# Operands of the second token half four steps sooner, early squares on ScalarE, and half an operand set loaded behind the weights

## The chip, the core and the metric

The kernel runs on one core of a Trainium2 chip. The metric is the time of one execution on the device in microseconds (us); a kernel's time is the median of its runs. The profile is of one execution of its own.

## The reference

One layer of a decoder trunk in float32, 1024 tokens, width 1024. Four token mixers (convolution, latent attention, pooling, gated spatial mixing) and an output projection give the residual `h`; all of this lies ahead of the change. What the change touches is the dense part behind it:

```
f = jnp.square(jax.nn.relu(rms_norm(h, ffn_norm_g) @ w_ff1))    # 1024 x 4096
h = h + f @ w_ff2                                               # 4096 x 1024
return rms_norm(h, final_norm_g)
```

## The kernel before

**Products.** Both matrix products are done by a scheme with seven products of half-size blocks instead of eight. A pair is 2 x 128 of the 4096 features (16 pairs); the tokens are cut in two halves of 512. For each pair the products P1 to P7 take one weight operand (`a11`, `a12`, `a21`, `a22` or sums of them, made in place by `sum1` to `sum4`) and one token operand: B11 and B21 (first half of the tokens), T1, B22, T2, T3, T4 (these need the second half). Each float32 operand is split into a high and a low part: ScalarE copies the high one (rounded to the matmul's type), VectorE subtracts for the low one, and a product is three matmul passes, so a step on TensorE is 4 x 3 = 12 matmuls of 128x512.

**Steps.** `run` writes the order of all engines out by hand. In iteration k it emits, in this order: the weight loads of step k+8 (SyncE), what follows step k-1 (`post`), the operand splits of step k+4 (`prep`), the extra work hung on step k (`now`), the second half of what follows step k-1 (`split`), and the matmuls of step k. Each engine runs its part of that list strictly in order. What lies ahead of step 0 is ordered by a planner and interleaves with the first steps.

**Phase one, early products.** Steps 0 to 23 are P1 (`one[p]`, step 2p-1) and P2 (`two[p-1]`, step 2p) of pairs 0 to 11, which need only the first token half, while the second half is still being finished. After `one[p]` ScalarE copies the bank out (`m1`, L980) and GpSimd's queue stores it; `two[p]`, three steps later, accumulates onto the same bank and so waits for that copy. After `two[p]`, `f_relu` takes Relu on ScalarE (L949), the square on VectorE (L951), stores `fe` to `fr`, and `f_parts` splits it into `fst` (L130, L131) and stores that to `fs` (L958). The tile `fst` is one single buffer ("CS") for pairs 0 to 2 and one of the ten weight slots (`w`) for pairs 3 to 11.

**Second-half operands.** They are hung on steps as `now` work, for j = 0 to 3: `hn_T1` at 7 + 2j (8 transposes on TensorE, L793; one ScalarE and four VectorE operations, L810 to L815), `hn_T1_split` at 8 + 2j (L825, L827: two copies, two subtractions), `combine` at 15 + 2j (two VectorE operations, L832, L833) and `combine_split` at 16 + 2j (three copies, three subtractions; the last copy takes the buffer that the third operand's source gives up). `h_away` at step 5 stores `h[4..7]` to HBM on SyncE's queue.

**The rest of phase one.** Step 24 is P5 of pair 0, step 25 P6, step 26 P3; P3 accumulates onto P5's bank and waits for ScalarE's copy `s5` of it, whose buffer ("N") held the last `fe`. Then come the other products of pairs 0 to 11, and all seven of pairs 12 to 15. The last seven steps (`tail`: P1, P5, P6, P2, P7, P3, P4 of pair 15) and the seven before them (`tail2`) also issue the first loads of phase two.

**Phase two.** Four chunks of four pairs, each with seven products M1, M2, M4, M6, M5, M7, M3 of four steps. Left operands are the stored parts `fop` 0, 1, 3 (from `fs`; M1, M2 and M4) or splits of the stored `f1`, `f2` (from `fr`); right operands are the second weights `w1`, `w2`. A step of M1 takes all four operands of a set. After each step VectorE adds the bank to `h` (`add_h`, L1083). The first loads, in SyncE's order, are `fop` 1, the last `w1`, `fop` 0, `w2`, `f1`, `f2`, then, hung on M2, `fop` 3.

The functions that the diff touches:

Of the kernel before, what the change touches and what calls it, by code (L numbers as in the profile page):

```python
# [11 lines left out]
AF = mybir.ActivationFunctionType  # L12
# [51 lines left out]
def trunk_kernel(tc, a):  # L64
    nc = tc.nc
    act = nc.scalar
    dve = nc.vector
    pool = nc.gpsimd
    pe = nc.tensor
    with (  # L70
        tc.tile_pool(name="sb", bufs=1) as sb,
        tc.tile_pool(name="ps", bufs=1, space=bass.MemoryType.PSUM) as ps,
        tc.tile_pool(name="hbm", bufs=1, space=bass.MemoryType.DRAM) as hbm,
    ):
        _trunk(tc, nc, act, dve, pool, pe, sb, ps, hbm, a)


def _trunk(tc, nc, act, dve, pool, pe, sb, ps, hbm, a):
# [25 lines left out]
    def wslot(name):  # L104
        return sb.tile([P, 1024], F32R, tag="w", name=name, bufs=2 * NW)

    def M(name, shape):
        return sb.tile([P] + shape, F32, tag="M", name=name, bufs=NM)
# [7 lines left out]
    def X(name):  # L116
        return ps.tile([P, 1024], F32, tag="X", name=name, bufs=2)
# [144 lines left out]
    b = X("zc")  # L262
# [40 lines left out]
    for i, hf in ((1, 0), (0, 1), (1, 1)):  # L303
        if (i, hf) == (0, 1):
            ba, bg = K("zc"), O("zc")
        else:
            b = X("zc")
# [37 lines left out]
    for i in range(2):  # L345
        w = load_w(a["w_cm"][4 + i], 1024, "wp%d" % i)
        b = X("zp")
# [434 lines left out]
    def split_to(t, src):  # L782
        split(t[:, 0], t[:, 1], src)
        return t
# [56 lines left out]
    def mm_half(b, w, name, start):  # L841

        for j in range(KH):
            mm3(b, lambda x: w[:, x, j * P:(j + 1) * P], lambda y: hb[name, j][:, y, :],
                start and j == 0, j == KH - 1, not start)

    def slot(name):
        return wslot(name).rearrange("p (x c) -> p x c", x=2)
# [4 lines left out]
    def E(name):  # L853
        return sb.tile([P, 512], F32, tag="e", name=name, bufs=1)
# [84 lines left out]
    def f_store(p, q, f):  # L939
        pool.dma_start(fr[p][q // 2][:, (q % 2) * 512:(q % 2 + 1) * 512], f)  # L940

    def f_sum(p, q, b, s):

        dve.tensor_add(s, b, s)  # L944
        dve.scalar_tensor_tensor(s, s, 0.0, s, ALU.max, ALU.mult)
        f_store(p, q, s)

    def f_relu(p, q, b, f, mul):
        act.activation(f, b, AF.Relu)  # L949
        if mul:  # L950
            dve.tensor_mul(f, f, f)  # L951
        else:
            act.activation(f, f, AF.Square)
        f_store(p, q, f)

    def f_parts(p, q, f, t):
        split_to(t, f)
        pool.dma_start(fs[p][q], t.rearrange("p x c -> p (x c)").bitcast(F32))  # L958

    def set_bank(b):  # L960

        pe.matmul(b, hb["B11", 0][:, 0, 0:P], hb["B11", 0][:, 0, :], start=True, stop=True)

    class Pair:
# [18 lines left out]
        def early(self):  # L983
            p = self.p
            o1, o2 = self.op("a11"), self.op("a12")

            def one():
                self.bx = (W, K, W, O)[p % 4]("ffe")
                mm_half(self.bx, o1.t, "B11", True)

            def one_post():
                self.keep("m1", lambda n: M(n, [512]), self.bx)
                pool.dma_start(m1[p], self.m1)

            def two():
                mm_half(self.bx, o2.t, "B21", False)

            def two_post():
                self.f = (N if p % 2 else E if p < NEARLY - 4 else spare)("fe")
                f_relu(p, 0, self.bx, self.f, True)  # L1000

            def two_split():
                f_parts(p, 0, self.f, slot("fst") if p > 2 else
                        sb.tile([P, 2, 512], F32R, tag="CS", name="fst", bufs=1))

            return (Step(one, [o1, o2], loads=[lambda: self.load(0)], post=one_post),
                    Step(two, post=two_post, split=two_split))
# [24 lines left out]
        def steps(self):  # L1032
            p, whole = self.p, self.p >= NEARLY
            S = {}

            def product(name, wop, bank, tok, start, **kw):
                o = self.op(wop)
                S[name] = Step(lambda: mm_half(bank(), o.t, tok, start), [o], **kw)

            def y0():  # L1040
                self.by = (K, O)[p % 2]("ffy")
                return self.by

            def x():
                return self.bx

            def z_seed():
                self.bz = X("ffz")[:, 0:512]
                if p < NEARLY + 2:
                    set_bank(self.bz)  # L1050
                act.activation(self.bz, self.bx, AF.Copy)

            def two_post():
                self.f11 = E("f11")
                f_relu(p, 0, self.bz, self.f11, False)

            def four_post():
                self.f21 = M("f21", [512])
                f_relu(p, 1, self.bx, self.f21, False)

            load = [lambda: self.load(0, "H"), lambda: self.load(1)]
            if whole:
                product("P1", "a11", x, "B11", True, loads=load, pre=self.banks, post=z_seed, sums=[self.sum1])
                load = []
                product("P2", "a12", lambda: self.bz, "B21", False, sums=[self.sum4], post=two_post,
                        split=lambda: f_parts(p, 0, self.f11, slot("fst")))
            product("P5", "a21", y0, "T1", True, loads=load, sums=[self.sum2],
                    post=lambda: self.keep("s5", (N, spare)[p % 2], self.by))
            product("P6", "a11", x, "T2", False, sums=[] if whole else [self.sum4],
                    post=lambda: self.keep("s2", lambda n: M(n, [512]), self.bx))  # L1070
            product("P3", "a12", lambda: self.by, "B22", False, sums=[] if whole else [self.sum3],
                    post=lambda: f_sum(p, 2, self.by, self.s2))
            product("P7", "a21", x, "T3", False, post=lambda: f_sum(p, 3, self.bx, self.s5),
                    split=lambda: f_parts(p, 3, self.s5, slot("fst")))
            product("P4", "a22", x, "T4", False, post=four_post, split=lambda: f_parts(p, 1, self.f21, slot("fst")))
            if whole:
                S["P2"].sums.append(self.sum3)
            self.S = S
# [393 lines left out]
    steps = [one[0]]  # L1472
# [1 line left out]
        steps += [one[p], two[p - 1]]  # L1474
    steps.append(two[-1])
    for j in range(KH):
        for f, s in ((hn_T1, 7 + 2 * j), (hn_T1_split, 8 + 2 * j), (combine, 15 + 2 * j), (combine_split, 16 + 2 * j)):
            steps[s].now.append(lambda j=j, f=f: f(j))
    steps[5].now.append(h_away)
    for p in pairs:  # L1480
        p.steps()

# [3 lines left out]
    for p in range(NPAIR):  # L1486
        s, nx = pairs[p].S, pairs[p + 1].S if p + 1 < NPAIR else {}
# [13 lines left out]
        pairs[p - 1].S["P7"].now.append(pairs[p].seed)  # L1501
    tail, tail2 = steps[-7:], steps[-14:-7]
    c0 = chunks[0]
    for t, n, name, ii in ((tail2, 1, "w1", (0, 1)), (tail2, 5, "w1", (2,)), (tail, 1, 1, range(4)),
                           (tail, 2, "w1", (3,)), (tail, 2, 0, range(4)), (tail, 3, "w2", range(4)),
                           (tail, 5, "f1", range(4)), (tail, 6, "f2", range(4))):
        t[n].now += [c0.ld(name, i) for i in ii]
    for n in range(4):
# [119 lines left out]
```

## Time and profile before

| | |
|---|---|
| time, median of 3 runs | 1042.67 us (1041.95 to 1043.56) |
| the profiled execution's own time | 1039.44 us |
| its span, first to last instruction | 1037.70 us |
| granted TensorE clock, mean | 0.985 |
| TensorE busy | 992.7 us |
| VectorE busy | 846.3 us |
| ScalarE busy | 502.3 us |
| TensorE waits and slow steps, 391 to 475 us | 2 long waits (3.61 and 2.79 us), one step at half clock |
| TensorE waits, 711 to 727 us | 0.43 and 1.93 us |

The profiled execution lies 3.23 us under the median; sums are made against it and then moved to the median. PE is TensorE, DVE VectorE, ACT ScalarE, POOL GpSimd, SP SyncE. A matmul is listed with its whole latency (0.39 us), while the next starts 0.23 us later.

### The profile page before, as it was taken

What the parts mean: (1) busy time and instruction counts of PE and PEld (TensorE: products, weight loads), DVE (VectorE), ACT (ScalarE), POOL (GpSimd) and SP (SyncE); (2) the same over time, 40 slices, a digit from 0 to 9 for tenths busy, and PEclk for the clock granted to TensorE, in tenths of its full rate; (3) what the DMA queues carried; (4) which work ended last, traced back from release to release, by engine and by line L of the source; (5) the groups of instructions that cost most, each with busy time, mean ns of one, the idle gap of its engine ahead of it and who ended that gap; (6) DMA issues with size and microseconds to landing.
All of it is one profiled execution on the core that took longest, in us unless ns stands there. A gap on an engine that the chain in (4) does not pass through costs nothing.

```text
span 1037.7 us, 13384 instructions
## 1 busy us (share of the span) xinstructions
PE 992.7 (96%) x4674; PEld 817.8 (79%) x4674; DVE 846.3 (82%) x1276; ACT 502.3 (48%) x937; POOL 246.8 (24%) x333
## 2 busy tenths in 40 slices
PE   9994899999999999988999999999999999999996
PEld 7883689888888887867888887887888888888885
DVE  5999999998888765987677775656998988988997
ACT  7641147556657765754545444453341431431424
POOL 0459558423232312222121111211000000000005
PEclk9997899999999999999999999999999999999998
DMA  9411015210002006866666675559858258258004
GB/s 334 165 56 37 32 54 185 82 41 23 19 1 82 1 1 216 298 246 219 235 217 230 233 235 185 220 181 414 337 189 298 82 181 306 81 180 326 1 1 163
DMA packets 49492, 165.71 MB, mean 160 GB/s; under 512 B 6032, under 2 KB 7952, under 8 KB 49424
## 3 DMA queue, kind: packets, MB, share of 16 engines
q1 hardware_dynamic: 36288, 119.68, 33.1%
q0 software_dynamic: 12992, 45.10, 11.1%
q8 instruction: 37, 0.61, 0.2%
q14 instruction: 31, 0.25, 0.1%
q10 hardware_dynamic: 144, 0.07, 0.0%
HBM read 113.45 MB, written 51.38 MB: 159 GB/s over the span
## 4 chain that ended last, share of the span: by engine, by line
PE 65%; DVE 16%; issue 6%; DMA 5%; ACT 4%; POOL 3%; SPq 0%; POOLq 0%; DVEq 0%; ACTq 0%
PE ffb L160 16%; PE ffx L160 13%; PE ffa L160 12%; DVE acc L337 8%; PE ffy L160 8%; PE wo L160 4%; PE ob L160 2%; PE s L676 2%; PE zc L160 2%; DMA raw_b<-in_w_ff 2%; DMA fs<-fst 1%; PE ptb L719 1%; PE woa L160 1%; PE qb L160 1%; DVE h L475 1%
## 5 line engine op out<-in xcount | busy, mean ns | idle before, releaser
L160 PE MATMUL ffb<-wop,fop 128*128 128x512 f32 x756 | 178.3, 395 | 0.0
L160 PEld LDWEIGHTS ffb<-wop,fop 128*128 128x128 f32 x756 | 142.1, 188 | 34.2
L160 PE MATMUL ffx<-hnT,wop 128*128 128x512 f32 x624 | 149.4, 392 | 0.8 <-DVE s L944 0.8
L160 PE MATMUL ffa<-wop,fop 128*128 128x512 f32 x576 | 137.3, 397 | 2.4 <-DVE h L1083 1.9
L160 PEld LDWEIGHTS ffx<-hnT,wop 128*128 128x128 f32 x624 | 117.0, 188 | 27.2 <-DVE s L944 1.2
L884 DVE TENSOR_TENSOR wop<-w_raw,wop 128x512 fp32r<-128x512 f32 x112 | 76.1, 688 | 68.3 <-ACT wop L881 68.3
L160 PEld LDWEIGHTS ffa<-wop,fop 128*128 128x128 f32 x576 | 109.2, 190 | 28.6 <-DVE h L1083 2.4
L881 ACT ACTIVATE wop<-raw_b 128x512 fp32r<-128x512 f32 x96 | 59.6, 623 | 122.9 <-PE ffa L160 44.3
L337 DVE SCALAR_TENSOR_TENSOR acc<-ycv,cols,acc 128x512 f32<-128x512 f32 (+22 forms) x100 | 99.1, 1032 | 0.7 <-ACT acc L317 0.4
L881 ACT ACTIVATE wop<-w_raw 128x512 fp32r<-128x512 f32 x112 | 68.8, 626 | 43.8 <-DVE w_raw L1027 18.9
L881 ACT ACTIVATE fop<-raw_f 128x512 fp32r<-128x512 f32 x64 | 39.8, 623 | 74.7 <-DVE h_back L1083 27.6
L160 PE MATMUL ffe<-hnT,wop 128*128 128x512 f32 x288 | 70.5, 402 | 4.4 <-ACT m L980 4.4
L1243 POOL TENSOR_SCALAR mr_ms<-mssq,epsr 128x1 f32<-128x1 f32 x7 | 2.8, 401 | 296.9 <-ACT fjunk L1241 296.9
L884 DVE TENSOR_TENSOR wop<-raw_b,wop 128x512 fp32r<-128x512 f32 x96 | 65.6, 684 | 9.3 <-ACT wop L881 8.6
L160 PEld LDWEIGHTS ffe<-hnT,wop 128*128 128x128 f32 x288 | 54.4, 191 | 17.0 <-ACT m L980 5.2
L160 PE MATMUL ffy<-hnB,wop 128*128 128x512 f32 x192 | 46.9, 393 | 2.8 <-ACT s L980 2.8
L160 PE MATMUL ffy<-hnT,wop 128*128 128x512 f32 x192 | 46.6, 391 | 0.0
L958 POOL DMA_DIRECT2D fs<-fst x48 | 25.8, 538 | 87.1 <-DVE fst L131 83.7
L160 PEld LDWEIGHTS ffy<-hnB,wop 128*128 128x128 f32 x192 | 36.0, 188 | 11.3 <-ACT s L980 3.2
L884 DVE TENSOR_TENSOR fop<-raw_f,fop 128x512 fp32r<-128x512 f32 x64 | 43.9, 686 | 0.0
L160 PEld LDWEIGHTS ffy<-hnT,wop 128*128 128x128 f32 x192 | 36.2, 189 | 8.1
L329 POOL TENSOR_TENSOR acc<-acc,tap 128x512 f32<-128x512 f32 (+7 forms) x20 | 35.0, 1749 | 28.9 <-ACT tap L328 27.6
(453 smaller groups left out, 2157.2 us busy)
## 6 DMA issues: line engine op xcount, KB each, us to landing
fs<-fst POOLq DMA_DIRECT2D x48, 512.0 KB, 3.4
fop<-fs SPq DMA_DIRECT2D x48, 512.0 KB, 7.2
w_raw<-in_w_ff SPq DMA_DIRECT2D x44, 512.0 KB, 4.4
raw_b<-in_w_ff SPq DMA_DIRECT2D x32, 512.0 KB, 5.9
raw_f<-fr SPq DMA_DIRECT2D x32, 512.0 KB, 5.7
fr<-s POOLq DMA_DIRECT2D x32, 256.0 KB, 3.2
fr<-f POOLq DMA_DIRECT2D x20, 256.0 KB, 2.4
xin<-in_x SPq DMA_DIRECT2D x8, 512.0 KB, 8.7
```

The source lines that it names most:

```text
L160: pe.matmul(out, lhs(x), rhs(y), start=start and i == 0, stop=stop and i == 2, skip_group_check=more)
L329: pool.tensor_tensor(aa, aa, tap, ALU.add)
L337: dve.scalar_tensor_tensor(aa, ya, c, aa, ALU.mult, ALU.add)
L475: dve.scalar_tensor_tensor(h[t], b, rs, h[t], ALU.mult, ALU.add)
L676: pe.matmul(sb_[:, c0:c0 + w], q[:, x, qo:qo + P], kt[:, y, 0:w], start=i == 0, stop=i == 2 and not last)
L719: pe.transpose(b[:, place[j] + s * P:place[j] + (s + 1) * P], pts[s][:, (2 * kp + j) * P:(2 * kp + j + 1) * P], ident)
L881: act.activation(self.t[:, 0], self.src(), AF.Copy)
L884: dve.tensor_sub(self.t[:, 1], self.src(), high(self.t))
L958: pool.dma_start(fs[p][q], t.rearrange("p x c -> p (x c)").bitcast(F32))
L1243: pool.tensor_scalar(ms, ssq, epsr[:, t:t + 1], 1.0, ALU.add, ALU.mult)
```

## The change

1. `f_relu` squares on ScalarE always; VectorE's multiplication (early pairs) goes.
2. `hn_T1` and `hn_T1_split` hang on steps 3 + 2j and 4 + 2j, `combine` and `combine_split` on 12 + 2j and 13 + 2j; `h_away` on step 4.
3. `fst` takes a weight slot from pair 1 on; only pair 0 uses "CS".
4. Of the four `fop` 1 loads, two are issued where all four were (`tail` step 1), two behind the four `w2` loads (`tail` step 3).

```
-    def f_relu(p, q, b, f, mul):
+    def f_relu(p, q, b, f):
         act.activation(f, b, AF.Relu)
-        if mul:
-            dve.tensor_mul(f, f, f)
-        else:
-            act.activation(f, f, AF.Square)
+        act.activation(f, f, AF.Square)
         f_store(p, q, f)
...
-                f_parts(p, 0, self.f, slot("fst") if p > 2 else
+                f_parts(p, 0, self.f, slot("fst") if p else
                         sb.tile([P, 2, 512], F32R, tag="CS", name="fst", bufs=1))
...
-        for f, s in ((hn_T1, 7 + 2 * j), (hn_T1_split, 8 + 2 * j), (combine, 15 + 2 * j), (combine_split, 16 + 2 * j)):
+        for f, s in ((hn_T1, 3 + 2 * j), (hn_T1_split, 4 + 2 * j), (combine, 12 + 2 * j), (combine_split, 13 + 2 * j)):
             steps[s].now.append(lambda j=j, f=f: f(j))
-    steps[5].now.append(h_away)
+    steps[4].now.append(h_away)
...
-    for t, n, name, ii in ((tail2, 1, "w1", (0, 1)), (tail2, 5, "w1", (2,)), (tail, 1, 1, range(4)),
-                           (tail, 2, "w1", (3,)), (tail, 2, 0, range(4)), (tail, 3, "w2", range(4)),
+    for t, n, name, ii in ((tail2, 1, "w1", (0, 1)), (tail2, 5, "w1", (2,)), (tail, 1, 1, (0, 1)),
+                           (tail, 2, "w1", (3,)), (tail, 2, 0, range(4)), (tail, 3, "w2", range(4)), (tail, 3, 1, (2, 3)),
                            (tail, 5, "f1", range(4)), (tail, 6, "f2", range(4))):
```

The callers of `f_relu` drop the last argument.

## Rows read from the trace of the kernel before

**Rows 1.** The page's first part: busy time, share of the span and instructions of each engine.

```profile
PE 992.7 (96%) x4674; PEld 817.8 (79%) x4674; DVE 846.3 (82%) x1276; ACT 502.3 (48%) x937; POOL 246.8 (24%) x333
```

**Rows 2.** Busy time by stretch: the stretch, its length, then busy us (and instructions) of each engine, TensorE's granted clock as a share of 2.4 GHz, the share of time that the DMA engines are busy, and GB/s. The two stretches are phase one behind the early products.

```profile
475.00:691.00 216.00, 215.22 (x938) 175.64 (x937) 145.41 (x225) 108.11 (x186) 41.49 (x77) 1.00 0.62 217
691.00:711.80 20.80, 20.80 (x92) 17.02 (x91) 13.23 (x21) 9.69 (x17) 4.30 (x8) 1.00 0.88 336
```

**Rows 3.** TensorE's timeline in the early products and the first two steps behind them: start, us from the first start to the last end, line, operation, what it writes and reads, how many, and in brackets the idle time before it and what ended it.

```profile
394.96 14.10 PE L160 MATMUL ffe<-hnT,wop 128*128 128x512 f32 x60 [0.74 <-ACT m L980]
408.90 1.04 PE L793 MATMUL htb<-ident,h 128*128 128x128 f32 x8
...
415.30 1.03 PE L793 MATMUL htb<-ident,h 128*128 128x128 f32 x8
...
428.88 27.85 PE L160 MATMUL ffe<-hnT,wop 128*128 128x512 f32 x120
460.35 4.62 PE L160 MATMUL ffe<-hnT,wop 128*128 128x512 f32 x12 [3.61 <-ACT m L980]
464.80 2.92 PE L160 MATMUL ffy<-hnT,wop 128*128 128x512 f32 x12
...
473.27 2.99 PE L160 MATMUL ffy<-hnB,wop 128*128 128x512 f32 x12 [2.79 <-ACT s L980]
```

**Rows 4.** Busy time by stretch, one microsecond behind the wait at 460.35 (columns as in rows 2; the granted clock is the 0.50).

```profile
462.00:463.00 1.00, 1.00 (x4) 0.81 (x3) 1.00 (x3) 0.06 (x1) 0.43 (x1) 0.50 0.16 62
```

**Rows 5.** The waits of 385 to 480 us: who waited, for whom; us in total, times, the longest.

```profile
ACT hnT L825 <- DVE hnT L827: 8.5, 4, 2.7
...
ACT fst L130 <- DMA fs<-fst: 6.7, 2, 5.1
```

**Rows 6.** VectorE's timeline, 385 to 478 us: the same operations of two neighbouring pairs, the two weight splits in the `hn_T1` stretch (L884) and the early `f_relu` in the combine stretch (L951).

```profile
419.90 1.29 DVE L884 TENSOR_TENSOR wop<-w_raw,wop 128x512 fp32r<-128x512 f32 x2
...
426.16 1.29 DVE L884 TENSOR_TENSOR wop<-w_raw,wop 128x512 fp32r<-128x512 f32 x2
...
444.41 0.68 DVE L951 TENSOR_TENSOR fe<-fe 128x512 f32<-128x512 f32 x1
...
450.74 0.69 DVE L951 TENSOR_TENSOR fe<-fe 128x512 f32<-128x512 f32 x1
```

**Rows 7.** TensorE's timeline at the start of phase two: M1 (`ffa`), then M2 and M4 (`ffb`).

```profile
711.82 2.20 PE L160 MATMUL ffa<-wop,fop 128*128 128x512 f32 x9
714.45 3.67 PE L160 MATMUL ffa<-wop,fop 128*128 128x512 f32 x15 [0.43 <-DMA fop<-fs]
720.04 7.36 PE L160 MATMUL ffa<-wop,fop 128*128 128x512 f32 x24 [1.93 <-DVE h L1083]
727.24 22.56 PE L160 MATMUL ffb<-wop,fop 128*128 128x512 f32 x96
```

**Rows 8.** The chain of work that ended last, 690 to 780 us: start, us, what.

```profile
700.46 16.22 DMA raw_b<-in_w_ff
...
719.24 0.76 DVE h L1083
```

**Rows 9.** ScalarE's timeline, 711.9 to 713.4 us: Relu and Square of a pair outside the early products, which already run there.

```profile
712.01 0.60 ACT L949 ACTIVATE f<-ffx 128x512 f32<-128x512 f32 x1 [1.88 <-PE ffx L160]
712.65 0.63 ACT L953 ACTIVATE f<-f 128x512 f32<-128x512 f32 x1
```

**Rows 10.** ScalarE's timeline, 385 to 478 us: the last scaling of an `h` tile of the second half, and two independent weight copies one behind the other.

```profile
396.33 1.15 ACT L757 ACTIVATE h<-h,rs 128x1024 f32<-128x1024 f32 x1
...
444.15 1.14 ACT L881 ACTIVATE wop<-w_raw 128x512 fp32r<-128x512 f32 x2
```

**Rows 11.** The DMA issues of the whole span: what, queue, operation, how many, KB of each, median us from issue to landing.

```profile
hs<-h SPq DMA_DIRECT2D x4, 512.0 KB, 10.6
```

**Rows 12.** The tile `fs` from 401 to 419 us: the three stores of `fst` that are issued there (pairs 0 to 2).

```profile
DMA to landing us min/median/max: 5.0/5.2/7.9
```

**Rows 13.** The chain of work that ended last, 300 to 560 us: the store of the last early pair.

```profile
469.37 3.15 DMA fr<-fe
```

**Rows 14.** Busy time by stretch at the start of phase two (columns as in rows 2; the last two are the DMA engines' share and GB/s).

```profile
694.00:697.00 3.00, 3.00 (x15) 2.44 (x14) 1.84 (x4) 2.28 (x4) 1.94 (x4) 1.00 0.85 213
697.00:712.00 15.00, 15.00 (x67) 12.30 (x66) 8.67 (x14) 6.18 (x11) 2.16 (x5) 1.00 1.02 410
...
730.00:746.00 16.00, 16.00 (x70) 12.88 (x70) 15.48 (x25) 4.73 (x8) 0.00 (x0) 1.00 1.03 409
```

**Rows 15.** SyncE's own waits ahead of its DMA issues, 697 to 741 us (columns as in rows 5).

```profile
SPq L1111 <- DMA fop<-fs: 10.0, 7, 2.5
```

**Rows 16.** The DMA issues of four moments, one each, with the us from issue to landing: issued at 698.93 (the eighth of SyncE's line from 693.42 on), 707.59 (the thirteenth), 716.75 (the eighteenth, the first `f2`) and 728.90 (the twenty-fifth, M4's last operand).

```profile
fop<-fs SPq DMA_DIRECT2D x1, 512.0 KB, 13.0
...
raw_b<-in_w_ff SPq DMA_DIRECT2D x1, 512.0 KB, 15.0
...
raw_f<-fr SPq DMA_DIRECT2D x1, 512.0 KB, 13.4
...
fop<-fs SPq DMA_DIRECT2D x1, 512.0 KB, 10.5
```

**Rows 17.** VectorE's timeline, 690 to 750 us: the first use of `f2`, and the last split of M4's weights.

```profile
730.16 0.69 DVE L1124 TENSOR_TENSOR raw_f<-raw_f,raw_f 128x512 f32<-128x512 f32 x1 [0.96 <-DMA raw_f<-fr]
...
739.64 0.69 DVE L884 TENSOR_TENSOR wop<-raw_b,wop 128x512 fp32r<-128x512 f32 x1
```

More of the change, by code (lines that the diff above doesn't have):

```diff
@@ L999, in two_post @@
                 self.f = (N if p % 2 else E if p < NEARLY - 4 else spare)("fe")
-                f_relu(p, 0, self.bx, self.f, True)
+                f_relu(p, 0, self.bx, self.f)
             def two_split():
-                f_parts(p, 0, self.f, slot("fst") if p > 2 else
+                f_parts(p, 0, self.f, slot("fst") if p else
                         sb.tile([P, 2, 512], F32R, tag="CS", name="fst", bufs=1))
@@ L1054, in two_post @@
                 self.f11 = E("f11")
-                f_relu(p, 0, self.bz, self.f11, False)
+                f_relu(p, 0, self.bz, self.f11)
             def four_post():
                 self.f21 = M("f21", [512])
-                f_relu(p, 1, self.bx, self.f21, False)
+                f_relu(p, 1, self.bx, self.f21)
             load = [lambda: self.load(0, "H"), lambda: self.load(1)]
```

## The prediction

> **What bounds the kernel now.** I read the page's first part, then busy time by stage, then TensorE's own timeline where a stage shows idle time, and for each idle stretch the waits and the other engines' timelines. TensorE is busy 96% of the span [rows 1], so only its gaps and slow stretches can give anything. From 475 to 711.8 us it has 0.8 us of gaps [rows 2]. The rest lies in two places.
>
> First place, the early products (391 to 475 us). Ten steps from 428.88 take 27.7 us, 2.77 each; the eleventh starts at 460.35, which is 3.77 late (3.61 of it recorded as a wait for ScalarE), and takes 4.45 us, 1.68 too long. Then TensorE waits 2.79 us before the product P3 [rows 3]. The slow step ran at a granted clock of 0.50, 1.2 GHz, after the idleness of 3.61 us [rows 4]; behind the 2.79 us no such stretch followed. The reader should see a backlog here, not one late operation. ScalarE stood 6.7 us for the store of `fst` (a single buffer for pairs 0 to 2) and 8.5 us for VectorE in `combine_split` [rows 5]. VectorE needs 6.26 us for two steps in the `hn_T1` stretch (419.90 to 426.16) and 6.33 in the combine stretch (444.41 to 450.74) [rows 6], where TensorE needs 6.40 with its transposes (408.90 to 415.30) and 5.54 without [rows 3]. So in the combine stretch VectorE falls back 0.8 us per pair of steps until TensorE catches up with it.
>
> Second place, the start of phase two. TensorE waits 0.43 us for a load of `fop` and 1.93 us for VectorE, and the 24 matmuls behind take 7.36 us, where two steps of 2.77 with the last one's tail take 5.7 [rows 7]. The chain of waits puts the 1.93 us down to one load: the first `w2` weights, issued at 700.46, landed 16.22 us later, and through the queues of ScalarE and VectorE they held `add_h` up until 720.0 [rows 8]. M2's first matmul comes at 727.24; four steps of 2.75 from 711.82 would have it at 722.8, 4.4 us sooner.
>
> **Part 1, squares on ScalarE.** Twelve VectorE multiplications of 0.69 us leave, one for each pair; two of them stand in [rows 6]. ScalarE does a Relu and 0.64 us later a Square of 0.63 [rows 9], so it has about 0.6 us more for each pair. What counts is the loop of the two engines, which I chain for the combine stretch with those durations, 0.53 us between independent operations of ScalarE (two take 1.14 us [rows 10]) and 0.61 of VectorE (two take 1.29 [rows 6]), from the Relu at r: Square r+0.64, two weight copies r+1.18 and r+1.70, copies for T2 and T3 r+2.22 and r+2.74; VectorE's two weight subtractions and those of T2 and T3 from r+1.85 until r+4.36; then T4's copy, which needs the buffer that T3's source gives up, r+4.40, `fst` r+4.93, `m1` r+5.46, next Relu r+5.94. That is 5.94 us instead of 6.33, still 0.4 over TensorE's 5.54: 1.2 us over three pairs, against a lead of two steps (5.5 us) with which `m1` is read out before its bank is used again.
>
> A rule of the Trainium skill speaks against this edit. ScalarE: Activation LUTs, section Rules for kernel authors, wants relu, max, min, add and mul on VectorE and not on ScalarE. By it the squares would stay, the pace would remain the row's 6.33 us, and the sum would lose 1.2 us over three combine pairs and as much over the closing ones: a gain smaller by some 2.4 us. The rows do not bear it out here: float32, 0.69 against 0.63 us, and VectorE is the fuller engine.
>
> **Part 2, second-half operands four steps sooner (combine three), `h_away` one.** The same work, 32 transposes and per pair of steps six VectorE operations (five in combine) and three of ScalarE, moves ahead. The last of `h[4..7]` is scaled by ScalarE at 396.33 + 1.15 = 397.48 [rows 10]; TensorE reaches step 3 at 394.96 + 2.77 = 397.73, so the transposes now placed there are ready by 0.25 us. If not, TensorE's queue stands behind them for the few ScalarE operations that the planner might put ahead, four of 0.6 us. On SyncE the four `hs` stores pass in front of one weight load, whose use is some 11 us after its issue; an `hs` store took 10.6 us to land [rows 11]. I take nothing; at worst ScalarE stands a few us, which the same lead hides. At the end VectorE no longer carries `combine` beside the preparation of P5 to P7. Pair 5's Relu follows TensorE at 428.9, pair 8's comes 3 x 5.94 later at 446.7; from there the same chaining gives `sum1` 451.8, Relu of pair 9 453.1, the copy of `a11` 454.6, `fst` 455.1, `m1` of pair 11 from 455.6 to 456.2, and TensorE wants its bank at 456.6. The 3.77 and the 1.68 us go, with 0.4 us to spare.
>
> **Part 3, `fst` of pairs 1 and 2 from the weight slots.** ScalarE's 6.7 us of standing goes [rows 5]. The price is ten slots that two more tiles share, each held until its store lands, 5.0 to 7.9 us [rows 12]. Below: nothing, since pairs 3 to 11 do this now, and the two waits of `fst` for a store are both in the single buffer. Above: two waits of 7.9 us. I take nothing, as the nearest rows are the same operation two pairs later.
>
> **Sum for the first place.** P5 starts at 464.80 - 3.77 - 1.68 = 459.35. P3 could start two steps (5.55 us) later, 464.9. It waits for ScalarE to copy `s5` out, into a buffer that is free when the store of pair 11's `fe` lands: Relu 460.1 (behind `fst` of pair 10), Square until 461.4, issue behind another store 461.9, landing 3.15 us on as now [rows 13], copy 0.6: P3 at 465.6, with 0.7 of the 2.79 us left. P3 moves from 473.27 to 465.6: **7.7 us**. TensorE is without gaps behind it [rows 2], so this is carried through phase one.
>
> **Part 4, half of the `fop` 1 loads behind the weights.** The DMA engines are full from 697 to 746 us, at 410 GB/s [rows 14], and SyncE's issues stood 10.0 us, in seven waits, for earlier `fop` loads to land [rows 15]. So a load lands by its place in the line. `w2`'s first is tenth now and becomes eighth: the eighth was issued at 698.93 and landed 13.0 us on, at 711.9, instead of 716.7 [rows 8, 16]. The last `fop` 0 becomes seventh and lands before that; M1 wants it at 713.9. Both waits of M1 vanish and M2 can start at 722.8. Of the two moved loads the later becomes thirteenth, 707.59 + 15.0 = 722.6 [rows 16], in time for M2's fourth operand (722.8 + 9 x 0.2333 = 724.9).
>
> But what is behind keeps its place: `f2` stays eighteenth, landing at 716.75 + 13.4 = 730.15, and M4's last operand load lands at 728.90 + 10.5 = 739.4 [rows 16]. VectorE takes `f2` up at 730.16 and needs until 739.64 + 0.69 = 740.33 to split M4's last weights [rows 17]. In the kernel before, 96 matmuls follow 727.24 without a wait in 22.56 us, 0.2333 each when the last one's tail of 0.16 is taken off; so M4 starts at 738.44 and comes to the last weights at 740.54 [rows 7]: 0.2 us to spare. With the change M4 starts at 722.8 + 11.2 = 734.0 and stands, in pieces, until 740.4. The 4.4 us won in M1 are given back in M4. Worth: nothing. If the granted clock falls after these pieces, up to 1.68 us as in the first place are lost, part of it under waits: I take -0.4.
>
> **Total.** 7.7 - 0.4 = 7.3 us. The profiled execution took 1039.44 us, 1.74 more than its span of 1037.70; it would take 1032.1. The median before lies 3.23 above the profiled run, so I forecast 1042.67 - 7.3 = **1035.4 us**, its own range 1033.5 to 1037.5. Under 0.2% (2.1 us) a change can't be told from none here.
>
> **Rivals.**
> 1. *Phase two keeps its gain.* If `f2` and M4's operands land sooner, M4 need not stand: 7.7 + 4.4 gives 1030.6. For it: from 694 to 697 the DMA engines have some air (0.85) [rows 14]. Against it: 49 full us behind.
> 2. *ScalarE becomes the pace*, as the one queue for relu, square, copies and `fst` that also stands for VectorE. At 6.4 us a pair instead of 5.94 it is 2.8 us further back after six pairs; the wait before the last early step returns at about 2 us and that before P3 in full. The gain is 3 to 5 us: 1039. For it: the 8.5 us of standing in `combine_split` [rows 5] stay in kind. Against it: the combine stretch ends three steps sooner.
> 3. *Slower: the weight slots.* If weights of pairs 5 to 7 get the slots of the moved `fst` tiles, ScalarE stands for stores that run beside `hs`: 2 x 7.9 = 15.8 us in place of 6.7 [rows 5, 12], 9.1 more; the shorter pairs save 2.5 and the early start 2, so about 4.6 us slower, 1047. It decides from some 11 us of standing on. Against it: ten slots, of which eight are in use then.
> 4. *No change.* A wait of 3 us and a slow step come back at P3 or in M4: 1041 to 1044.
>
> The skill's rule above would lead to rival 2.
>
> **Chances.** Forecast 0.55, rivals 0.13, 0.18, 0.07 and 0.07. Faster: 0.55 + 0.13 + 0.17 = 0.85; same: 0.01 + 0.07 = 0.08; slower 0.07. Range 1030.3 to 1040.5: the first two cases and nearly all of rival 2.
>
> **What would show it.** Part 1: no `fe` multiplication on VectorE, twelve more Squares. Part 2: first transposes near 397.8 without a TensorE wait, P5 near 459.4 and no granted clock of 0.50 ahead of it. Part 3: no ScalarE wait for the store of `fst`. Part 4: M1 without a wait, M2 some 11 us after M1, then TensorE idle in M4's first step, whose last group starts 28.7 us after M1 as now. I am wrong if TensorE waits for `m1` or before P3 as long as now, if ScalarE waits for slots between steps 5 and 11, or if M4 runs without a wait.

## The result, and the profile after

The changed kernel takes **1032.22 us** (median of 4 runs, 1031.83 to 1034.43), the kernel before 1042.31 beside it (4 runs, 1041.26 to 1043.56): a ratio of 0.9907 [0.9889, 0.9925], 10.1 us. The forecast was 1035.4, range 1030.3 to 1040.5. The time lies inside that range, but under the range of the forecast's own case, 1033.5 to 1037.5. Four runs of the kernel before, in which TensorE's mean granted clock was 0.556 to 0.846, are left out of the medians and ratios below.

The page's first part: TensorE's busy time stays at that of [rows 1], VectorE has twelve instructions fewer, ScalarE twelve more.

```profile
PE 992.1 (96%) x4674; PEld 817.6 (79%) x4674; DVE 838.7 (81%) x1264; ACT 509.9 (49%) x949; POOL 249.4 (24%) x333
```

Lines of the code behind `f_relu` stand three lower than before (L980 is L977 now). TensorE's timeline from step 2 to P3 (start, us, line, operation, count, idle time before it and what ended it), to be held against [rows 3]:

```profile
397.31 3.04 PE L160 MATMUL ffe<-hnT,wop 128*128 128x512 f32 x12 [0.74 <-ACT m L977]
400.19 1.04 PE L793 MATMUL htb<-ident,h 128*128 128x128 f32 x8
...
420.17 41.66 PE L160 MATMUL ffe<-hnT,wop 128*128 128x512 f32 x180
461.67 2.90 PE L160 MATMUL ffy<-hnT,wop 128*128 128x512 f32 x12
...
467.74 2.55 PE L160 MATMUL ffy<-hnB,wop 128*128 128x512 f32 x10 [0.40 <-ACT s L977]
```

The transposes come four steps sooner and find their operands ready. Fifteen steps follow without a wait, 2.77 us each. The 3.61 us before the last early step and the slow step behind it are gone, and 0.40 of the 2.79 us before P3 are left. From step 2 to P3 it is 70.43 us now and 78.31 before.

The start of phase two, the same view, against [rows 7]:

```profile
706.29 11.04 PE L160 MATMUL ffa<-wop,fop 128*128 128x512 f32 x48
717.17 11.36 PE L160 MATMUL ffb<-wop,fop 128*128 128x512 f32 x48
731.06 4.01 PE L160 MATMUL ffb<-wop,fop 128*128 128x512 f32 x9 [2.53 <-DMA fop<-fs]
735.31 0.51 PE L160 MATMUL ffb<-wop,fop 128*128 128x512 f32 x1 [0.24 <-ACT wop L881]
736.04 9.13 PE L160 MATMUL ffb<-wop,fop 128*128 128x512 f32 x38 [0.22 <-DVE wop L884]
745.01 11.36 PE L160 MATMUL ffa<-wop,fop 128*128 128x512 f32 x48
```

M1 runs through and M2 starts 10.88 us behind it (15.42 before). Then M4 stands, and the next product, M6, starts 38.72 us after M1, where it was 37.82: phase two gives back all it won and 0.9 us more. Between P3 and M1 both profiles take 238.55 us.

**Why 10.1 and not 7.3 us.** The two profiled executions do not start alike. Busy time by stretch, from 5 to 15 us of both (columns as in rows 2), the kernel before first:

```profile
5.00:15.00 10.00, 9.52 (x38) 7.07 (x39) 8.49 (x16) 8.11 (x16) 0.00 (x0) 1.00 1.01 365
```

```profile
5.00:15.00 10.00, 8.39 (x27) 6.25 (x28) 8.27 (x16) 7.54 (x15) 0.00 (x0) 0.83 0.98 331
```

In work that the change does not touch, the changed kernel's execution waited 1.32 us for a copy of ScalarE, where the kernel before waited 0.18, and then ran at 1.2 GHz for some 3.4 us (0.83 over 10 us):

```profile
7.92 0.79 PE L160 MATMUL zc<-xT_h,wcm1h 128*128 128x512 f32 x1 [1.32 <-ACT wcm1h L130]
```

It reached step 2 2.35 us later (397.31 against 394.96). From that step to the end it took 635.4 us, the kernel before 642.7: **7.35 us, forecast 7.3**. The sum agrees better than its terms: 7.88 us are won up to P3 (forecast 7.7), 0.90 are lost between M1 and M6 (forecast 0.4), and 0.37 are won behind M6, nearly all of them after the start of TensorE's last product, where the forecast had nothing.

The profiled execution of the changed kernel took 1034.43 us, 2.2 *above* its median; that of the kernel before lay about 3 *below* its median. The other 2.7 us of the medians are not in these two traces. The interval of the ratio, 7.8 to 11.6 us, leaves room for less; the first and the fourth experiment repeat both kernels.

### The profile page after: what moved, and what is told of

Same layout as the page of the kernel before. It is cut to its first block, busy times and chain, and to the rows that moved or that the text cites. A ratio compares the mean times of both kernels' runs of the same rounds, so it can differ in the third digit from the quotient of the medians.

```text
span 1032.7 us, 13375 instructions
## 1 busy us (share of the span) xinstructions
PE 992.1 (96%) x4674; PEld 817.6 (79%) x4674; DVE 838.7 (81%) x1264; ACT 509.9 (49%) x949; POOL 249.4 (24%) x333
## 4 chain that ended last, share of the span: by engine, by line
PE 69%; DVE 15%; DMA 5%; ACT 4%; issue 4%; POOL 2%; SPq 0%; POOLq 0%; DVEq 0%; ACTq 0%
PE ffb L160 15%; PE ffx L160 13%; PE ffa L160 11%; PE ffy L160 8%; DVE acc L337 7%; PE wo L160 4%; PE ffe L160 4%; PE ob L160 2%; PE zc L160 2%; PE s L676 2%; DMA raw_f<-fr 1%; DMA raw_b<-in_w_ff 1%; PE ptb L719 1%; PE woa L160 1%; PE qb L160 1%
## 5 line engine op out<-in xcount | busy, mean ns | idle before, releaser
L160 PE MATMUL ffb<-wop,fop 128*128 128x512 f32 x756 | 180.8, 398 | 3.0 <-DMA fop<-fs 2.5
L884 DVE TENSOR_TENSOR wop<-w_raw,wop 128x512 fp32r<-128x512 f32 x112 | 76.1, 688 | 78.5 <-ACT wop L881 78.3
L160 PE MATMUL ffa<-wop,fop 128*128 128x512 f32 x576 | 135.1, 393 | 0.0
L337 DVE SCALAR_TENSOR_TENSOR acc<-ycv,cols,acc 128x512 f32<-128x512 f32 (+22 forms) x100 | 97.0, 1011 | 0.7 <-ACT acc L317 0.4
L881 ACT ACTIVATE wop<-w_raw 128x512 fp32r<-128x512 f32 x112 | 68.7, 625 | 42.3 <-DVE w_raw L1024 18.9
L884 DVE TENSOR_TENSOR wop<-raw_b,wop 128x512 fp32r<-128x512 f32 x96 | 65.5, 682 | 5.6 <-ACT wop L881 5.0
L884 DVE TENSOR_TENSOR fop<-raw_f,fop 128x512 fp32r<-128x512 f32 x64 | 43.7, 683 | 0.0
```

Source lines behind the costliest of these rows:

```text
L160: pe.matmul(out, lhs(x), rhs(y), start=start and i == 0, stop=stop and i == 2, skip_group_check=more)
L337: dve.scalar_tensor_tensor(aa, ya, c, aa, ALU.mult, ALU.add)
L881: act.activation(self.t[:, 0], self.src(), AF.Copy)
L884: dve.tensor_sub(self.t[:, 1], self.src(), high(self.t))
```

## The experiments

Each kernel was timed against the kernel before on the same chip. Three times recur, read as in the fences above: step 2 to P3 (78.31 before, 70.43 after), P3 to M1 (238.55 in both), M1 to M6 (37.82, 38.72).

**The kernel before, once more.** No edit.

> The kernel before, unchanged, for a second profile of it. The gain by medians (10.1 us) is 2.7 us more than the gain between the two profiles counted from step 2 on (7.35 us). Theory A, the states of single executions: the profiled execution of before had a start at full clock and no half clock behind the wait at P3, most executions have one or the other; then this profile shows a time of 1041 to 1043.5 and a half-clock stretch of about 1.7 us that the first profile lacks, either within the first 15 us or behind a wait at P3 near 473 us. Theory B, part 4 is worth 2.7 us more in timed runs than in the profile: then this profile shows longer waits than 0.43 and 1.93 us at the start of phase two.

Measured: 0.9991 [0.9979, 1.0003]; its own runs went from 1039.27 to 1044.67 us. Step 2 to P3 took 78.36, M1 to M6 37.76, as in the first profile, but the span was 1042.9 against 1037.7. TensorE's timeline at P3, and busy time by stretch behind it:

```profile
476.86 4.60 PE L160 MATMUL ffy<-hnB,wop 128*128 128x512 f32 x12 [2.89 <-ACT s L980]
```

```profile
478.00:479.00 1.00, 1.00 (x3) 0.79 (x3) 0.69 (x3) 0.33 (x1) 0.00 (x0) 0.50 0.55 217
```

After 2.89 us of idleness P3 ran at 1.2 GHz and took 4.60 us; in the first profile it took 2.99 after 2.79 us [rows 3]. P3 to M1 is 1.59 us longer for it, and the start of the kernel 3.54 us. At the start the recorded clock does not show the loss: it reads 1.00, while TensorE starts 23 matmuls in the stretch in which the first profile has 38 and the changed kernel's, at 0.83, has 27.

```profile
5.00:15.00 10.00, 8.85 (x23) 6.54 (x24) 8.37 (x16) 7.55 (x15) 0.00 (x0) 1.00 0.97 325
```

Theory B fell, as M1's waits were 0.40 and 1.93 us. The stretch of theory A is there, at both places instead of one, so this execution took more than the expected 1041 to 1043.5 us. The waits of this kernel repeat to 0.1 us between these two profiles (in the run of part 4 alone, whose early products are the same, they are 4.28 and 1.92 us), but whether a slow stretch follows one does not, and the first profile had caught few of them. It also has the earliest step 2 of all fourteen traces, 394.96 against 395.20 to 398.50. The change takes away all but 0.40 us of the wait before P3 too, and with it this place. The granted clock over the whole of a run points the same way: 0.979 to 0.986 in 22 runs of the kernel before on this chip, 0.987 to 0.989 in the four of the changed one. The timed runs have no trace, so which stretches each of them had stays open. Nor is a median of a few runs exact: the ten runs here and the others of the same kernel beside them have medians of 1040.53 and 1041.96 us, 1.4 us apart.

**Part 4 alone.**

```diff
-    for t, n, name, ii in ((tail2, 1, "w1", (0, 1)), (tail2, 5, "w1", (2,)), (tail, 1, 1, range(4)),
+    for t, n, name, ii in ((tail2, 1, "w1", (0, 1)), (tail2, 5, "w1", (2,)), (tail, 1, 1, (0, 1)),
...
-                           (tail, 2, "w1", (3,)), (tail, 2, 0, range(4)), (tail, 3, "w2", range(4)),
+                           (tail, 2, "w1", (3,)), (tail, 2, 0, range(4)), (tail, 3, "w2", range(4)), (tail, 3, 1, (2, 3)),
```

> The kernel before with part 4 alone (half of the fop 1 loads behind w2). My theory, the line of loads and VectorE's work behind f2 pin M4: M1 runs without a wait, M2 starts 10.9 us after M1, then TensorE stands some 4 us in M4's first step; time 0 to 1.5 us longer than before, ratio 1.000 to 1.0015. Rival 1, phase two keeps its gain: 4.4 us shorter, ratio 0.996; a gain of 2.7 us (0.9974) would put the surplus of the result here.

Measured: 1.0001 [0.9991, 1.0012]. TensorE's timeline in phase two:

```profile
714.76 11.04 PE L160 MATMUL ffa<-wop,fop 128*128 128x512 f32 x48
725.64 11.36 PE L160 MATMUL ffb<-wop,fop 128*128 128x512 f32 x48
739.03 0.93 PE L160 MATMUL ffb<-wop,fop 128*128 128x512 f32 x3 [2.03 <-DMA fop<-fs]
...
753.00 11.36 PE L160 MATMUL ffa<-wop,fop 128*128 128x512 f32 x48
```

Both waits of M1 are gone, and M6 still comes 38.24 us after M1. Two removed waits and a slow step are worth nothing.

**Everything but part 4** (the diff above, undone in the changed kernel).

> The changed kernel with the old order of the loads, parts 1 to 3 kept. My theory: ratio to before 0.990 to 0.992, that is the same time as the changed kernel or up to 1 us less; waits of 0.43 and 1.93 us in M1 come back, M4 starts without a wait. Rival 1: 2.7 to 4.4 us longer than the changed kernel, ratio 0.993 to 0.995.

Measured: 0.9912 [0.9897, 0.9926].

```profile
705.96 2.20 PE L160 MATMUL ffa<-wop,fop 128*128 128x512 f32 x9
708.64 3.68 PE L160 MATMUL ffa<-wop,fop 128*128 128x512 f32 x15 [0.48 <-DMA fop<-fs]
714.22 5.74 PE L160 MATMUL ffa<-wop,fop 128*128 128x512 f32 x24 [1.90 <-DVE h L1080]
719.79 13.46 PE L160 MATMUL ffb<-wop,fop 128*128 128x512 f32 x57
733.86 0.51 PE L160 MATMUL ffb<-wop,fop 128*128 128x512 f32 x1 [0.60 <-ACT wop L881]
...
743.56 11.36 PE L160 MATMUL ffa<-wop,fop 128*128 128x512 f32 x48
```

M1 has its two waits back and M6 comes 37.60 us after it, 1 us *sooner* than with part 4. The 24 matmuls behind the 1.90 us took 5.74 us here, not the 7.36 of [rows 7]: no slow step followed this time. So M2 started 13.83 us after M1 instead of 15.42, but only 0.2 of these 1.6 us reach M6, since M4 then waits for its weights (0.60 us), against the expectation that it would not wait. What pins M4 is there in the old order of loads, too.

**The changed kernel, once more.** No edit.

> The changed kernel, unchanged, beside the other two on one chip. Ratio 0.9907 as before; its profile with a start at full clock takes 1032.1, with one at half clock 1034.4.

Measured: 0.9918 [0.9905, 0.9931] (1033.31 us, 1041.96 for the kernel before). Step 2 to P3 70.46, M1 to M6 38.57, and 635.2 us from step 2 to the end (635.4 in the first profile). By the ratio the gain is 8.5 us here, with an interval of 7.2 to 9.9, which holds the 7.35 us of the first two traces. Between the two repeated profiles it is 9.2 us from step 2 on (644.4 and 635.2), of which 1.59 are the slow stretch at P3. All that part 4 does to the time is between this and the run above: 0.9912 and 0.9918, within each other's interval.

**Without part 1.** The squares of early pairs go back to VectorE.

```diff
-        act.activation(f, f, AF.Square)
+        if p < NEARLY and q == 0:
+            dve.tensor_mul(f, f, f)
+        else:
+            act.activation(f, f, AF.Square)
```

> The changed kernel with the early squares back on VectorE. From step 2 to P3 before takes 78.3 us, the changed kernel 70.4. Theory, a loop of two engines with VectorE the fuller: the pace goes back to about 6.3 us per pair in the combine stretch, a wait for m1 of up to 1 us and one of 1.5 to 2.5 us before P3 return, 72 to 73 us, ratio 0.993 to 0.994. Rival, ScalarE is the pace (the rule that keeps mul on VectorE): 70.4 us or less, ratio 0.991 or lower.

Measured: 0.994 [0.9919, 0.996]. ScalarE's timeline, the Relus of two neighbouring pairs in the combine stretch, first without part 1 and then in the changed kernel:

```profile
441.86 0.59 ACT L949 ACTIVATE fe<-ffe 128x512 f32<-128x512 f32 x1
...
448.18 0.59 ACT L949 ACTIVATE fe<-ffe 128x512 f32<-128x512 f32 x1
```

```profile
443.25 0.59 ACT L949 ACTIVATE fe<-ffe 128x512 f32<-128x512 f32 x1
443.88 0.63 ACT L950 ACTIVATE fe<-fe 128x512 f32<-128x512 f32 x1
...
449.13 0.59 ACT L949 ACTIVATE fe<-ffe 128x512 f32<-128x512 f32 x1
...
457.91 0.58 ACT L977 ACTIVATE m<-ffe 128x512 f32<-128x512 f32 x1
```

A pair takes 6.32 us without the move and 5.88 with it. The last line is the readout of pair 11. Without the move TensorE waits for that readout, and as long as with it before P3:

```profile
458.14 3.04 PE L160 MATMUL ffe<-hnT,wop 128*128 128x512 f32 x12 [0.40 <-ACT m L980]
...
467.10 3.00 PE L160 MATMUL ffy<-hnB,wop 128*128 128x512 f32 x12 [0.43 <-ACT s L980]
```

P3 comes 71.11 us after step 2, 0.7 later than with the move. That lies between the two expectations: the wait for `m1` came back, the longer wait before P3 did not. The intervals of 0.994 and 0.9918 overlap, so the move's worth rests on the traces.

**Part 3 alone.**

```diff
-slot("fst") if p > 2 else
+slot("fst") if p else
```

> The kernel before with the fst of pairs 1 and 2 in weight slots, nothing else. Theory, the backlog comes from several causes: ScalarE's 6.7 us of standing go, but VectorE still carries the squares and the combine work beside the preparation of P5 to P7: the wait before the last early step shrinks to 0 to 2 us, that before P3 stays: 74 to 77 us from step 2 to P3, ratio 0.994 to 0.998. Rival, the single buffer alone made the backlog: 70.4 us, ratio 0.992. Rival, weights stand for slots: ScalarE waits for stores in steps 5 to 11, 78 us or more.

Measured: 0.9987 [0.9978, 0.9997].

```profile
458.96 3.03 PE L160 MATMUL ffe<-hnT,wop 128*128 128x512 f32 x12 [0.87 <-ACT m L980]
...
471.88 4.48 PE L160 MATMUL ffy<-hnB,wop 128*128 128x512 f32 x12 [4.34 <-ACT s L980]
```

The wait before the last early step falls from 3.61 to 0.87 us and its slow step goes; the wait before P3 grows from 2.79 to 4.34, and a slow step follows there. P3 is 2.8 us sooner by the trace, and 1.3 us are left by the ratio.

**Without part 2** (`hn_T1` and `combine` at their old steps).

```diff
-((hn_T1, 3 + 2 * j), (hn_T1_split, 4 + 2 * j), (combine, 12 + 2 * j), (combine_split, 13 + 2 * j))
+((hn_T1, 7 + 2 * j), (hn_T1_split, 8 + 2 * j), (combine, 15 + 2 * j), (combine_split, 16 + 2 * j))
...
-    steps[4].now.append(h_away)
+    steps[5].now.append(h_away)
```

> The changed kernel with the second-half operands and h_away back at their old steps. Theory, what counts is that combine no longer lies beside the preparation of P5 to P7: 72 to 75 us from step 2 to P3, with a wait before P3 of 1.5 to 3 us, ratio 0.993 to 0.996. Rival, the earlier steps are worth nothing once parts 1 and 3 are there: 70.4 us, ratio 0.991.

Measured: 1.0006 [0.999, 1.0022]. TensorE's timeline, and one row of the waits of 385 to 480 us (who, for whom, us in total, times, longest):

```profile
458.47 3.04 PE L160 MATMUL ffe<-hnT,wop 128*128 128x512 f32 x12 [1.50 <-ACT m L977]
...
472.03 5.13 PE L160 MATMUL ffy<-hnB,wop 128*128 128x512 f32 x12 [4.71 <-ACT s L977]
```

```profile
ACT hnT L825 <- DVE hnT L827: 8.0, 4, 2.7
```

With the squares moved and no store to wait for, ScalarE still stands 8.0 us in `combine_split`, as in [rows 5], and TensorE 1.50 and 4.71 us. P3 comes after 76.83 us, which is more than the theory's 72 to 75. Parts 1 and 3 (part 4 is in this kernel too) give nothing that can be measured without part 2.

**Part 2 alone** (the diff above the other way round, in the kernel before).

> The kernel before with part 2 alone (second-half operands and h_away at the earlier steps); squares on VectorE, one fst buffer for pairs 0 to 2, old order of loads. Theory now: part 2 carries nearly all of the first place, since VectorE and ScalarE are then done with combine before the preparation of P5 to P7: 70.5 to 72 us from step 2 to P3 (before 78.3, changed kernel 70.4), ratio 0.992 to 0.994. Rival, the parts only work together, as each takes a piece of one backlog: 73 to 76 us, ratio 0.995 to 0.998.

Measured: 0.9937 [0.9914, 0.9961].

```profile
459.92 3.03 PE L160 MATMUL ffe<-hnT,wop 128*128 128x512 f32 x12 [1.03 <-ACT m L980]
...
468.89 2.99 PE L160 MATMUL ffy<-hnB,wop 128*128 128x512 f32 x12 [0.45 <-ACT s L980]
```

P3 comes after 71.77 us: 6.5 of the 7.9 us are part 2's own, though ScalarE here still stands 5.5 us in two waits for the store of `fst`.

**Without part 3** (its diff above, undone in the changed kernel).

> The changed kernel with the fst of pairs 0 to 2 in the single buffer again. Theory: ScalarE stands about 5 to 7 us for its store in steps 5 to 8, now ahead of hn_T1_split; the backlog is 3 to 5 us larger when the combine stretch begins and part of it is left at the end: 71.5 to 74 us from step 2 to P3, ratio 0.992 to 0.995. Rival, the earlier start swallows it: 70.4 us, ratio 0.991.

Measured: 0.9928 [0.991, 0.9947]; P3 after 70.46 us, not a tenth later than with part 3. A row of the waits of 385 to 480 us:

```profile
ACT fst L130 <- DMA fs<-fst: 4.3, 1, 4.3
```

The standing is there, and TensorE does not notice it: the rival came, and not the expected 71.5 to 74 us.

**Only `combine` sooner** (`hn_T1` at steps 7 and 8, `h_away` at 5, `combine` at 12 and 13).

```diff
-((hn_T1, 3 + 2 * j), (hn_T1_split, 4 + 2 * j), (combine, 12 + 2 * j), (combine_split, 13 + 2 * j))
+((hn_T1, 7 + 2 * j), (hn_T1_split, 8 + 2 * j), (combine, 12 + 2 * j), (combine_split, 13 + 2 * j))
```

> The changed kernel with only combine and combine_split at the earlier steps; hn_T1, hn_T1_split and h_away at the old ones. If it is the end of the early stretch that counts (combine out of the way of P5 to P7): 70.4 to 71.5 us from step 2 to P3. If it is the early start that counts (VectorE's air in steps 3 to 6 used): 73 to 77 us with a wait before P3 of 2 to 4 us, as without part 2 (76.8).

Measured: 0.9954 [0.9935, 0.9974]; P3 after 73.77 us.

```profile
444.89 14.45 PE L160 MATMUL ffe<-hnT,wop 128*128 128x512 f32 x60 [1.44 <-ACT m L977]
460.03 3.04 PE L160 MATMUL ffe<-hnT,wop 128*128 128x512 f32 x12 [0.69 <-ACT m L977]
...
469.24 3.03 PE L160 MATMUL ffy<-hnB,wop 128*128 128x512 f32 x12 [0.68 <-ACT s L977]
```

The `combine` steps alone bring 3.1 of the 6.4 us (76.83 to 73.77), the early `hn_T1` the other 3.3, in this order: with `hn_T1` up to step 14 and `combine` from step 12 on, the two stretches overlap, and the lead of two steps is used up at 444.89. The time fits the expectation for the early start, but its wait of 2 to 4 us before P3 was 0.68. `hn_T1` alone sooner, and `h_away` by itself, were not run.

**Half of each first `f1` load left out**, to test what pins M4.

```diff
-                    nc.sync.dma_start(t.rearrange("p x c -> p (x c)"), src(pp[i]))
+                    if c == 0 and names[0] == "f11":
+                        nc.sync.dma_start(t[:, 0], src(pp[i])[:, 0:512])
+                        pool.memset(t[:, 1], 0.0)
+                    else:
+                        nc.sync.dma_start(t.rearrange("p x c -> p (x c)"), src(pp[i]))
```

> The changed kernel with the first chunk's f1 loads halved: only their first 512 columns are loaded, the other half is set to zero by GpSimd, so part of the second product is left out. 1 MB less stands ahead of f2 and fop 3 in SyncE's line, 2.6 us at 410 GB/s. Theory, the line of loads and VectorE's work behind f2 set M4 and M6: from M1 to M6 35 to 36.5 us instead of 38.6, time 2 to 3.5 us shorter than the changed kernel. Rival, TensorE itself or the half clock sets it: 38 us or more.

Measured: 0.9899 [0.9881, 0.9916]. The first use of `f2` on VectorE, and TensorE's M1 and M6:

```profile
721.59 0.69 DVE L1125 TENSOR_TENSOR raw_f<-raw_f,raw_f 128x512 f32<-128x512 f32 x1 [3.03 <-DMA raw_f<-fr]
```

```profile
705.71 11.04 PE L160 MATMUL ffa<-wop,fop 128*128 128x512 f32 x48
...
740.78 11.36 PE L160 MATMUL ffa<-wop,fop 128*128 128x512 f32 x48
```

Four loads ahead of `f2` carry half their bytes; `f2` is taken up 15.88 us after M1 instead of 19.53, and M6 comes 35.07 after M1 instead of 38.72. The ratio is 2 us better than the 0.9918 of the changed kernel on another chip, with intervals that overlap, so this reading, too, rests on the trace.

**M4's operand loads ahead of `f2`.**

```diff
-(tail, 5, "f1", range(4)), (tail, 6, "f2", range(4))):
+(tail, 5, "f1", range(4)), (tail, 6, 3, range(4)), (tail, 6, "f2", range(4))):
...
-                now("M2", n, self.ld(3, n))
+                if not first:
+                    now("M2", n, self.ld(3, n))
```

> The changed kernel with the first chunk's fop 3 loads ahead of f2 instead of behind it, nothing left out. M4's last operand then lands 5.1 us sooner, f2 5.1 us later. If VectorE's work behind f2 is the pin: M4's first step waits for VectorE and ScalarE, not for a load, and M6 comes some 5 us later: M1 to M6 43 to 44 us instead of 38.6, time about 5 us longer than the changed kernel. If the landing of M4's operand is the pin: M4 starts without a long wait, M1 to M6 35 to 36 us, time about 3 us shorter.

Measured: 0.9986 [0.9975, 0.9997].

```profile
729.08 0.69 DVE L1121 TENSOR_TENSOR raw_f<-raw_f,raw_f 128x512 f32<-128x512 f32 x1 [11.73 <-DMA raw_f<-fr]
```

```profile
704.49 11.04 PE L160 MATMUL ffa<-wop,fop 128*128 128x512 f32 x48
...
731.87 2.90 PE L160 MATMUL ffb<-wop,fop 128*128 128x512 f32 x6 [5.14 <-ACT wop L881]
...
738.66 12.25 PE L160 MATMUL ffb<-wop,fop 128*128 128x512 f32 x39 [1.46 <-ACT wop L881]
750.75 11.36 PE L160 MATMUL ffa<-wop,fop 128*128 128x512 f32 x48
```

M4 no longer waits for its operands but for its weights, which VectorE prepares behind `f2`, and `f2` comes 5.1 us later (24.59 after M1 against 19.53). So the wait for a `fop` load that the trace of the changed kernel names is only the first of two; behind it stand `f2` and VectorE's work. M6 comes 46.26 us after M1. That is more than the 43 to 44 us expected. The granted clock stood at 0.50 from M4's first matmul until 744.7, and the 39 matmuls from 738.66 on took 12.25 us, 3.0 more than at 0.2333 us each:

```profile
741.00:742.00 1.00, 1.00 (x4) 0.81 (x3) 1.00 (x3) 0.12 (x1) 0.00 (x0) 0.50 0.11 45
```

## Why the prediction was right, and where its sizes were off

**First place: right to 0.2 us.** With the 2.35 us by which the profiled execution was late at step 2 added to each forecast, P5 was to start at 461.70 (measured 461.67), the Relu of pair 9 at 455.45 (455.39), the readout of pair 11 to end at 458.55 (458.49) and P3 to start at 467.95 (467.74). The chained loop of ScalarE and VectorE, 5.94 us a pair, was 5.88 in the trace. The wait left before P3 was 0.40 us, forecast 0.7, and its cause the forecast one, the landing of pair 11's store.

**Whose gain it is: told apart by the runs, not by the sum.** The forecast gave one sum for parts 1 to 3. Part 2 is worth 6.5 us by itself. Part 1, reckoned at 1.2 us over the combine stretch and as much at the end, is worth 0.7 us when it is taken away from the whole, and part 3, which removes 4.3 us of standing, nothing; both together make the 1.3 us between 71.77 and 70.43. They overlap: with part 2 there, part 1 gives 1.3 us without part 3 (70.46), part 3 gives 0.7 without part 1 (71.11), and part 3 on top of part 1 gives nothing. The lead of two steps that the prediction itself names fits this: in the run without part 3 ScalarE stands 4.3 us for a store, less than the lead of 5.5 us, and TensorE does not wait. The forecast, right in total, put too much on part 1. Part 1 alone was not run.

**The rule on squares.** The Trainium skill (ScalarE: Activation LUTs, section Rules for kernel authors) wants multiplications on VectorE. Here, in float32, both traces speak against it: 0.63 us a Square on ScalarE, 0.69 a multiplication on VectorE, and a pair of steps 0.44 us shorter with the move.

**Phase two: mechanism right, size off.** The forecast was that the 4.4 us won in M1 are given back in M4, pinned at 28.7 us after M1, and that 0.4 us more go to the clock. The runs of part 4 alone and of all but part 4 show the first; the last two experiments show the pin, and rival 1 fell. The loss was 0.9 us, and not by the clock. The granted clock did fall to 0.50 in M4's first step,

```profile
732.00:733.00 1.00, 1.00 (x4) 0.59 (x3) 1.00 (x2) 0.00 (x0) 0.00 (x0) 0.50 1.01 401
```

but TensorE waited for M4's weights behind it (0.24 us at 735.31, 0.22 at 736.04), so the slow matmuls cost nothing. The 0.9 us are there because the pin moved; that the 0.4 set aside for the clock covers a part of them is luck. This is VectorE's timeline in the changed kernel, the first use of `f2` and the last split of M4's weights, against [rows 17], and the link of the chain that ended last which brings `f2`:

```profile
725.82 0.69 DVE L1121 TENSOR_TENSOR raw_f<-raw_f,raw_f 128x512 f32<-128x512 f32 x1 [6.67 <-DMA raw_f<-fr]
...
735.29 0.69 DVE L884 TENSOR_TENSOR wop<-raw_b,wop 128x512 fp32r<-128x512 f32 x1
```

```profile
711.28 14.52 DMA raw_f<-fr
```

`f2` was issued 4.99 us after M1 (4.93 before) but took 14.5 us to land instead of 13.4 [rows 16], and the split ended 29.7 us after M1. The step "`f2` stays eighteenth, landing at" the same distance failed: the place stayed, the time from issue to landing did not. In the profiles with part 4 (the last two experiments apart) `f2` is taken up 18.9 to 19.5 us after M1, in those without it 18.3 to 18.7. Why the landing is longer behind the new order was not settled.

**Standing of ScalarE.** As forecast, no wait for the store of `fst` is left. The wait for VectorE in `combine_split`, put at staying "in kind", fell from 8.5 us in four waits to 3.8. Rival 2, with ScalarE as the pace, did not come: fifteen steps without a wait. Rival 3 did not come either; the weight slots cost nothing.

**From the profile to the median: a term that is not fixed.** The forecast took the 3.23 us between the profiled run and the median of the kernel before as fixed. They are not: the changed kernel's profiled run lay 2.2 us above its median, and the second one of the kernel before 4.1 above the median of its ten runs. 7.35 us are what the first two traces show the same work to take less; the other 2.7 us were not in the sum at all. Part of them may be stretches at 1.2 GHz, since the change removes places where they can follow (1.59 us at P3 in the repeated profile), but the timed runs have no trace. Part may be the spread of the runs, since the repeat gave 8.5 us and not 10.1. How the 2.7 us divide stays open. The measured 1032.22 us lies nearer to rival 1's 1030.6 than to 1035.4; that the mechanism was the forecast's and not that of rival 1 is told by the traces, not by the time.

## What to carry to other kernels

Where two engines of a pipeline fall behind by a little in every step, move the work to a stretch that still has a lead, and only then ask what shaving operations or removing waits is worth; here moving gave 6.5 us in the trace and the other two 1.3 together. Before a stall is removed, look for what is pinned behind it by its place in a full line of loads: a wait that is gone there comes back a product later. And hold one profiled execution against the spread of the runs before its total is carried over, since stretches at the lower clock behind the same waits come and go.

## What was not expected of the hardware

The same wait is followed by a granted clock of 0.50, the lower of the two levels, in one execution and not in another: 2.79 us before P3 without it, 2.89 us with it, in one and the same kernel; 1.93 us in M1 with it [rows 7], 1.90 us without it in the run of all but part 4. The start of the kernel, too, differs: step 2 came 2.35 us later than in the first profile with a granted clock of 0.50 recorded on the way, and 3.54 later with matmuls 0.43 us apart, as at 0.50, while the recorded clock read 1.00. So the pace of the matmuls has to be read beside the recorded clock. What decides the level no run here shows.
